# A decoder block on one core: the FFN's down projection as seven block products instead of eight, its left-hand sums made beside gate/up, and tiles aligned to 512 bytes

## The chip, the core and the metric

The kernel is one program for one core of a Trainium2 chip. The metric is device time of one execution in microseconds. All matrix products of the part that is changed are done in three passes: each f32 operand is split into a rounded part (`h`, type float32r) and the rest (`l`), and `h*h + h*l + l*h` is accumulated, so one 128x512 result of a contraction over 128 costs three matrix multiplications.

## The reference, cut to what matters

```
u = rms_norm(h, attn_norm_g);  h = h + hybrid_mixer(u, ...)      # two attention mixers, merged
u = rms_norm(h, ffn_norm_g)
h = h + (silu(u @ w_gate) * (u @ w_up)) @ w_down                 # 1024x1024 @ 1024x2816, then 1024x2816 @ 2816x1024
out = rms_norm(h, final_norm_g)
```

There are 1024 tokens, the model is 1024 wide and the FFN 2816 wide.

## The kernel before, in words

The kernel runs in stages: the attention mixers (until about 870 us), the branch projections and the output projection (until about 1047 us), the transposes that make the FFN's input (until about 1110 us), gate/up (until 1506 us), down (until 1748 us), and the last output tiles. A scheduler of the framework orders each engine's instructions by a simulated timeline; buffers in pools set how far a stage may run ahead. The order below the source is therefore not the order on the engines.

Gate/up (`Pair`, lines 1139 to 1221) is done already as 2x2x2 block products with seven multiplications: the tokens' halves and the model's halves of the input lie on chip as the eight tiles B11, B21, B22 and T1 to T4, and each `Pair` makes four results of 128 FFN columns x 512 tokens. `operand` (L1125) splits a block on ScalarE (L1128) and VectorE (L1129). What is gated, `sl` (L1183), goes to DRAM as `hhd`, 44 stores of 256 KB from GpSimd's queue (L1184). The two weights are loaded as `raw`, 128x8x256, rows of 1 KB (L1063).

Down (L1291 to L1329) is a plain product. Two halves of 512 tokens (`th`); in each, 22 steps over the FFN's 128-column slices. A step loads 128 rows of `w_down` (`wdr`, 512 KB) and the gated slice (`hr`, 256 KB), splits both (L1258 on ScalarE, L1259 on VectorE) and issues 24 matrix multiplications (L1308 to L1310) into all eight PSUM banks. Both halves load `w_down` anew. When a half is complete, the eight banks are added to the residual `hf` (L1318), the squares are summed (L1320), and the normalised tile is stored (L1327, L1329). `hf` has three buffers, so a fourth tile's load (L1314) waits until an earlier one's stores have landed.

The pools named `lined` pad each tile to a multiple of 128 bytes, and the pool `eps` at the right end of the memory holds 24 floats (96 bytes), which shifts all that lies left of it in right-hand pools. As allocated, the matrix multiplications of gate/up, down, branch and output projection have both operands at a remainder of 384 bytes to 512. Those of the merge gates and extra projections (`mg`, lines 314 to 338: 18 blocks x 2 halves x 24, 864 in all, 512 columns each) have the moving operand at remainder 384 and the stationary one at 0. The projections of 384 columns have 0 and 384.

## Time and profile before

| | us |
|---|---|
| median of 3 runs | 1773.97 (1773.64 to 9481.85) |
| profiled execution, device time | 1771.06 |
| its span | 1769.3 |
| granted TensorE clock, mean over the span | 0.982 |
| TensorE (PE) busy | 1681.4 (95%) |
| VectorE (DVE) busy | 1009.7 (57%) |
| ScalarE (ACT) busy | 753.5 (43%) |

The profile's page gives busy times over the whole span; a matrix multiplication is counted until its modelled end, so two that follow each other overlap in it, and the pace of a stage is read from the starts. Other views are the stretches (busy time and count of each engine between two times), the timeline of an engine, the groups of instructions, the chain of waits that ended last, and the DMA issues with the time until they landed. Times are from the span's start.

### The profile page before, as it was taken

Reading aid. Unit: us, or ns where it says so; the run is one execution under the profiler, and the core shown is the slowest. Engines: PE = TensorE matmul, PEld = TensorE weight load, DVE = VectorE, ACT = ScalarE, POOL = GpSimd, SP = SyncE. Lnnn points to the kernel's source line nnn. Section 1 sums busy time; section 2 is a strip of 40 time slices with the busy share of each in tenths; the row PEclk is TensorE's granted clock in tenths of the full one; section 3 lists DMA queues with packets and bytes.
Section 4 is the critical chain, followed back from the end, with each engine's and each line's share of the span. In section 5 each row is a group of like instructions: output and inputs, shape, how many; then the busy total and the mean of one; then the engine's idle time right before and its main releaser. Section 6 shows DMA issues by size and latency. Waiting matters only on the chain.

```text
span 1769.3 us, 24833 instructions
## 1 busy us (share of the span) xinstructions
PE 1681.4 (95%) x9157; PEld 1446.5 (82%) x9157; DVE 1009.7 (57%) x1974; ACT 753.5 (43%) x1574; POOL 436.5 (25%) x601
## 2 busy tenths in 40 slices
PE   5999999999999999999999988999999999998995
PEld 4888888887889989998888866888888888786884
DVE  8554645455358678888654177655555554335434
ACT  4334343344333268878643144433333332234323
POOL 4432323233122356657444020000000000001001
PEclk8999999999999999999999989999999999999998
DMA  6120211013223010100474320432222220545542
GB/s 204 45 78 24 78 44 58 30 47 106 73 74 87 14 31 26 39 16 21 145 246 150 107 95 30 137 107 84 78 95 72 78 96 36 196 143 178 174 144 82
DMA packets 120361, 157.90 MB, mean 89 GB/s; under 512 B 10208, under 2 KB 90112, under 8 KB 120240
## 3 DMA queue, kind: packets, MB, share of 16 engines
q1 hardware_dynamic: 111936, 132.50, 23.9%
q0 software_dynamic: 7120, 23.29, 3.4%
q8 instruction: 72, 1.18, 0.3%
q10 hardware_dynamic: 1184, 0.53, 0.1%
q14 instruction: 49, 0.40, 0.1%
HBM read 120.64 MB, written 35.65 MB: 88 GB/s over the span
## 4 chain that ended last, share of the span: by engine, by line
PE 84%; DVE 8%; ACT 4%; DMA 2%; issue 1%; POOL 1%; SPq 0%; ACTq 0%; DVEq 0%; POOLq 0%
PE mm L1135 8%; PE mm L1136 8%; PE mm L1137 8%; PE b L158 6%; PE b L159 6%; PE b L160 6%; PE s L874 3%; PE mm L1308 3%; PE mm L1309 3%; PE mm L1310 3%; PE b L927 3%; PE b L938 3%; PE s L158 2%; PE s L159 2%; PE s L160 2%; PE br L160 2%
## 5 line engine op out<-in xcount | busy, mean ns | idle before, releaser
L1184 POOL DMA_DIRECT2D hhd<-sl x44 | 23.9, 544 | 438.6 <-DVE sl L1183 438.6
L158 PE MATMUL b<-uh,mg_h 128*128 128x512 f32 x288 | 115.8, 402 | 0.7 <-ACT mg_st L337 0.7
L159 PE MATMUL b<-ul,mg_h 128*128 128x512 f32 x288 | 114.7, 398 | 0.0
L160 PE MATMUL b<-uh,mg_l 128*128 128x512 f32 x288 | 113.9, 395 | 0.0
L1128 ACT ACTIVATE oh<-S 128x512 fp32r<-128x512 f32 x88 | 55.6, 632 | 131.1 <-PE mm L1136 114.2
L874 PE MATMUL s<-kN,qN 128*128 128x320 f32 (+5 forms) x384 | 100.7, 365 | 3.6 <-ACT p L891 2.6
L1309 PE MATMUL mm<-wdl,hdh 128*128 128x512 f32 x264 | 102.7, 389 | 0.0
L1310 PE MATMUL mm<-wdh,hdl 128*128 128x512 f32 x264 | 102.5, 389 | 0.0
L1259 DVE TENSOR_TENSOR hdl<-hr,hdh 128x512 fp32r<-128x512 f32 x44 | 30.5, 692 | 120.1 <-ACT hdh L1258 117.3
L942 DVE TENSOR_TENSOR pl<-b,ph 128x512 fp32r<-128x512 f32 (+1 forms) x152 | 90.6, 613 | 12.8 <-ACT ph L941 11.8
L159 PE MATMUL b<-pw_l,uh 128*128 128x384 f32 x256 | 88.5, 346 | 6.6 <-DVE pw_l L269 6.6
L1258 ACT ACTIVATE hdh<-hr 128x512 fp32r<-128x512 f32 x44 | 27.8, 631 | 156.5 <-PE tp L1309 137.1
L941 ACT ACTIVATE ph<-b 128x512 fp32r<-128x512 f32 (+1 forms) x152 | 80.3, 545 | 31.7 <-PE b L938 30.4
L891 ACT ACTIVATE p<-s,mn 128x640 f32<-128x640 f32 (+7 forms) x128 | 89.3, 703 | 7.6 <-DVE sm L892 2.5
L158 PE MATMUL b<-pw_h,uh 128*128 128x384 f32 x256 | 89.7, 350 | 1.8 <-ACT uh L217 1.2
L898 POOL TENSOR_TENSOR p<-p,sm 128x640 f32<-128x640 f32 (+3 forms) x64 | 89.2, 1416 | 2.5
L160 PE MATMUL b<-pw_h,ul 128*128 128x384 f32 x256 | 88.4, 345 | 1.4 <-DVE ul L218 1.4
L1128 ACT ACTIVATE oh<-raw 128x512 fp32r<-128x512 f32 x66 | 41.6, 632 | 109.4 <-PE mm L1136 108.2
L1129 DVE TENSOR_TENSOR ol<-S,oh 128x512 fp32r<-128x512 f32 x88 | 60.4, 686 | 43.7 <-PE mm L1137 25.7
L938 PE MATMUL b<-ident,p 128*128 128x128 f32 x528 | 83.0, 275 | 1.4 <-POOL p L895 0.6
L465 DVE TENSOR_REDUCE mn<-s 128x1 f32<-128x128 f32 (+7 forms) x64 | 46.0, 753 | 55.4 <-PE s L464 55.3
L158 PE MATMUL s<-pw_h,uh 128*128 128x256 f32 (+1 forms) x256 | 74.9, 293 | 2.6 <-ACT xs L648 1.6
(387 smaller groups left out, 5187.8 us busy)
## 6 DMA issues: line engine op xcount, KB each, us to landing
wdr<-in_w_down_dram SPq DMA_DIRECT2D x44, 512.0 KB, 3.6
raw<-in_w_gate_dram SPq DMA_DIRECT2D x11, 1024.0 KB, 5.3
raw<-in_w_up_dram SPq DMA_DIRECT2D x11, 1024.0 KB, 5.3
hhd<-sl POOLq DMA_DIRECT2D x44, 256.0 KB, 2.3
hr<-hhd SPq DMA_DIRECT2D x44, 256.0 KB, 2.6
mg_raw<-in_w_in_dram SPq DMA_DIRECT2D x18, 512.0 KB, 4.6
mgd<-mg_st POOLq DMA_DIRECT2D x32, 256.0 KB, 3.7
sg<-mgd SPq DMA_DIRECT2D x16, 512.0 KB, 5.1
```

Source lines behind the costliest of these rows:

```text
L158: T.matmul(ps, ah, bh, start=(i == 0), stop=False)
L159: T.matmul(ps, ah, bl, start=False, stop=False)
L160: last = T.matmul(ps, al, bh, start=False, stop=(i == n - 1))
L874: T.matmul(s_[:, c], qN[:, 2 * hp + es[c * len(es) // 2], i * 128:(i + 1) * 128], kNs[br][:, v, g, c0:c0 + cw], start=(v == 0), stop=(v == 1))
L938: T.transpose(tp[:, 2 * (b - b0) + e], p[:, e, b * 128:(b + 1) * 128], ident)
L942: V.tensor_sub(pl[:, :nt], tp[:, :nt], ph[:, :nt])
L1128: A.activation(wh, src, AF.Copy)
L1135: T.matmul(ps, w[0][:, k], b[0][:, k], start=(first and k == 0), stop=False, **kw)
L1136: T.matmul(ps, w[0][:, k], b[1][:, k], start=False, stop=False, **kw)
L1137: T.matmul(ps, w[1][:, k], b[0][:, k], start=False, stop=(k == 3), **kw)
L1309: T.matmul(ps, hh[:, ts], dl[:, cs], start=False, stop=False)
L1310: T.matmul(ps, hl[:, ts], dh[:, cs], start=False, stop=(f == NF - 1))
```

## The change

Four things are done.

- **Down as seven block products.** The 1024x2816 gated matrix is cut into 2x2 blocks (token halves x FFN halves) and `w_down` into 2x2 blocks (FFN halves x column halves). Seven products of 11 steps each (`PRODUCTS`) are accumulated into two sets of four banks in turn, `bx` and `by`; a step splits one 128x512 piece of each side and issues 12 matrix multiplications. Partial results that two outputs share are copied out of PSUM by ScalarE (`kept`) and added later by VectorE (`settle`). The right-hand sums (`make`) are made on VectorE in place, in 33 of the 77 steps and for a later product.
- **The left-hand sums beside gate/up.** `gated_sums` makes S1 to S4 from the gated blocks, four VectorE operations for each of 11 pairs of `Pair`s, and stores seven blocks instead of four: 77 stores of 256 KB. For this a `Pair` takes FFN columns p and p+11, so `raw` is loaded in two DMAs with rows of 512 bytes.
- **`w_down` on chip.** Each of its four blocks is loaded once and stays: block 00 during gate/up, 01 and 11 into the place of B11 to B22, 10 into a pool of its own. The eight residual tiles `hf` are all on chip before the last products. The left-hand pieces `ar` come back from DRAM with two buffers.
- **Alignment.** `lined` pads to 512 bytes, `epst` holds 120 floats (480 bytes), small tiles of the first mixer go to a pool `das`. As allocated, both operands of the matrix multiplications named above are at remainder 0. The order of all engines up to the FFN's input stays the same.

The diff, cut to its core:

```diff
@@ -118,9 +118,9 @@
         def tile(self, shape, dtype, **kw):
             n = math.prod(shape[1:])
             size = 2 if dtype == BF else 4
-            if n * size % 128 == 0:
+            if n * size % 512 == 0:
                 return self.p.tile(shape, dtype, **kw)
-            t = self.p.tile([shape[0], -(-n * size // 128) * 128 // size], dtype, **kw)[:, :n]
+            t = self.p.tile([shape[0], -(-n * size // 512) * 512 // size], dtype, **kw)[:, :n]
...
-    epst = eps_pool.tile([128, 24], F32, name="epst")[:, 0:1]
+    epst = eps_pool.tile([128, 120], F32, name="epst")[:, 0:1]
...
             kT = st["kT", h]
-            mn = da.tile([128, 2], F32, name="mn")
-            sm = da.tile([128, 2], F32, name="sm")
-            rc = da.tile([128, 16], F32, name="rc")[:, 0:2]
+            mn = das.tile([128, 2], F32, name="mn")
+            sm = das.tile([128, 2], F32, name="sm")
...
 
-    hh_dram = [tc.dram_tile((128, S), F32, name="hhd%d" % i) for i in range(NF)]
+    HF = NF // 2
+    A_BLOCKS = ("A00", "A01", "A11", "S1", "S2", "S3", "S4")
...
         raws[n] = ffr.tile([128, KD, 256], F32, name="raw", bufs=2)
-        nc.sync.dma_start(raws[n], (w_gate, w_up)[b][:, p * 256:(p + 1) * 256].rearrange("(k p) n -> p k n", p=128))
+        for r in range(2):
+            c0 = (p + r * HF) * 128
+            nc.sync.dma_start(raws[n][:, :, r * 128:r * 128 + 128],
+                              (w_gate, w_up)[b][:, c0:c0 + 128].rearrange("(k p) n -> p k n", p=128))
...
     tres = fres.enter_context(ExitStack())
+    ff = ctx.enter_context(lined("ff", side="right"))
     tb_ = tres.enter_context(pool("tb", side="right"))
-    ff = tres.enter_context(lined("ff", side="right"))
     for nm in ("T1", "T2", "T3", "T4"):
         B[nm] = [tb_.tile([128, 4, 512], R, name="B%s%s" % (nm, v)) for v in "hl"]
 
     def operand(src):
-        wh = ff.tile([128, 4, 128], R, name="oh", bufs=4)
-        wl = ff.tile([128, 4, 128], R, name="ol", bufs=4)
+        wh = ff.tile([128, 4, 128], R, name="oh", bufs=6)
+        wl = ff.tile([128, 4, 128], R, name="ol", bufs=6)
         A.activation(wh, src, AF.Copy)
         V.tensor_sub(wl, src, wh)
...
             if not self.up:
-                sl = ff.tile([128, 512], F32, name="sl", bufs=5)
+                sl = gated_tile()
...
                 V.tensor_mul(sl, sl, ps if m is None else m)
-                nc.gpsimd.dma_start(hh_dram[2 * self.p + r][:, c * 512:(c + 1) * 512], sl)
+                self.gated_sums("A%d%d" % (c, r), sl)
+
+        def gated_sums(self, nm, t):
+
+            g = self.g
+            g[nm] = t
+
+            def store(k):
+                nc.gpsimd.dma_start(hh_dram[k][self.p], g[k])
+
+            if nm != "A10":
+                store(nm)
+            if nm == "A10":
+                g["S3"] = gated_tile()
+                V.tensor_sub(g["S3"], g["A00"], g["A10"])
+                store("S3")
+            elif nm == "A11":
+                g["S1"] = g["A10"]
+                V.tensor_add(g["S1"], g["A10"], g["A11"])
+                store("S1")
+                g["S2"] = gated_tile()
+                V.tensor_sub(g["S2"], g["S1"], g["A00"])
+                store("S2")
+            elif nm == "A01":
+                g["S4"] = gated_tile()
+                V.tensor_sub(g["S4"], g["A01"], g["S2"])
+                store("S4")
 
...
             self.done(1, 0, self.ps["X"], None)
+
+    late = []
+
+    def gated_tile():
+        if not late:
+            return ff.tile([128, 512], F32, name="sl0")
+        return late[0].tile([128, 512], F32, name="sl", bufs=7)
 
...
+    late.append(dn)
+    BW = {"00": [dn.tile([128, 512], F32, name="b00_%d" % p) for p in range(HF)]}
+
+    def load_block(nm, p):
+        r, c = int(nm[0]), int(nm[1])
+        nc.sync.dma_start(BW[nm][p], w_down[(p + r * HF) * 128:(p + r * HF + 1) * 128, c * 512:(c + 1) * 512])
...
             load_pair(n + 2)
+        if n >= NF - HF:
+            load_block("00", n - (NF - HF))
...
@@ -1288,45 +1318,131 @@
     tres.close()
 
 
...
+    dr = ctx.enter_context(pool("dr", side="right"))
+    quads = [ub.tile([128, 4, 512], F32, name="q" + nm, tag=nm)
+             for nm in ("B11h", "B11l", "B21h", "B21l", "B22h", "B22l")]
+    blocks = [t[:, i] for t in quads for i in range(4)]
+    BW["01"], BW["11"] = blocks[:HF], blocks[HF:2 * HF]
+    gO = flat(quads[5][:, 2:4])
+    BW["10"] = [dr.tile([128, 512], F32, name="b10_%d" % p) for p in range(HF)]
+    hf = [dr.tile([128, D], F32, name="hf%d" % t) for t in range(NT)]
+    ssq = dr.tile([128, NT, 2], F32, name="ssq")
+    bx = [fp.tile([128, 512], F32, name="tp", bufs=2) for _ in range(2)] + [mm_bank() for _ in range(2)]
+    by = [mm_bank() for _ in range(4)]
+
+    PRODUCTS = (("A00", "00", None, None, bx), ("S1", "00", ("01", "00"), "01", by),
+                ("S2", "00", ("11", "00"), "11", bx), ("S4", "11", None, None, by),
+                ("S3", "01", ("11", "01"), None, bx), ("A01", "10", None, "10", by),
+                ("A11", "00", ("10", "00"), None, bx))
+    GRP = 3
+    raw_a, ops = {}, {}
+    NS = len(PRODUCTS) * HF
+
+    def fetch(n):
+        i, p = divmod(n, HF)
+        if PRODUCTS[i][3]:
+            load_block(PRODUCTS[i][3], p)
+        raw_a[n] = dn.tile([128, 512], F32, name="ar", bufs=2)
+        nc.sync.dma_start(raw_a[n], hh_dram[PRODUCTS[i][0]][p])
+
+    def split(src):
+        h = ff.tile([128, 512], R, name="oh", bufs=6)
+        l = ff.tile([128, 512], R, name="ol", bufs=6)
+        A.activation(h, src, AF.Copy)
+        V.tensor_sub(l, src, h)
+        return h, l
+
+    def prepare(n):
+        i, p = divmod(n, HF)
+        _, nm, make, _, _ = PRODUCTS[i]
+        a = split(raw_a.pop(n))
+        w = BW[nm][p]
+        if make:
+            V.tensor_sub(w, BW[make[0]][p], BW[make[1]][p])
+        ops[n] = a + split(w)
+
+    def step(n, tbs):
+        i, p = divmod(n, HF)
+        ah, al, wh, wl = ops[n]
+        fresh = i in (0, 1, 5) and p == 0
+        kw = {} if i in (0, 1, 5) else dict(skip_group_check=True)
+        for tb in tbs:
+            ts = slice(tb * 128, (tb + 1) * 128)
+            ps = PRODUCTS[i][4][tb]
+            T.matmul(ps, ah[:, ts], wh, start=fresh, stop=False, **kw)
+            T.matmul(ps, ah[:, ts], wl, start=False, stop=False, **kw)
+            T.matmul(ps, al[:, ts], wh, start=False, stop=(p == HF - 1), **kw)
+
+    def kept(banks, places):
+        out_ = []
+        for tb in range(4):
+            pl, nm, bufs = places[tb]
+            out_.append(pl.tile([128, 512], F32, name=nm, bufs=bufs))
+            A.activation(out_[tb], banks[tb], AF.Copy)
+        return out_
+
+    def settle(t, c, bank_, part):
+
+        hc = hf[t][:, c * 512:c * 512 + 512]
+        if part is None:
+            V.tensor_add(hc, hc, bank_)
+        else:
+            V.tensor_add(part, bank_, part)
+            V.tensor_add(hc, hc, part)
+        sq = ff.tile([128, 512], F32, name="S", bufs=3)
+        A.activation(sq, hc, AF.Square, accum_out=ssq[:, t, c:c + 1])
+
+    def finish(t):
+        V.tensor_add(ssq[:, t, 0:1], ssq[:, t, 0:1], ssq[:, t, 1:2])
+        r = rsqrt(dr, [128, 1], ssq[:, t, 0:1], 1.0 / D, "fin")
+        rows = slice(t * 128, (t + 1) * 128)
+        h0, h1 = hf[t][:, 0:512], hf[t][:, 512:1024]
+        V.scalar_tensor_tensor(h0, h0, r, gO[:, 0:512], op0=OP.mult, op1=OP.mult)
+        nc.sync.dma_start(out[rows, 0:512], h0)
+        V.scalar_tensor_tensor(h1, h1, r, gO[:, 512:1024], op0=OP.mult, op1=OP.mult)
+        nc.sync.dma_start(out[rows, 512:1024], h1)
+
+    for n in range(2):
+        fetch(n)
+    prepare(0)
+    keep = {}
+    for n in range(NS):
+        i, p = divmod(n, HF)
+        if n + 2 < NS:
+            fetch(n + 2)
+        if n == HF:
+            nc.sync.dma_start(gO, bcast_rows(final_norm_g, D))
+        if i in (2, 4) and p < 4:
+            t = p + (0 if i == 2 else 4)
+            nc.sync.dma_start(hf[t], hx_dram[t])
+        if n + 1 < NS:
+            prepare(n + 1)
+        if n < NS - GRP:
+            step(n, range(4))
+        elif n == NS - 1:
             for tb in range(4):
...
+                for m in range(NS - GRP, NS):
+                    step(m, (tb,))
+                settle(tb + 4, 0, bx[tb], None)
+                finish(tb + 4)
+        if p < HF - 1:
+            continue
+        if i == 0:
+            keep["m1"] = kept(bx, [(dn, "sl", 7)] * 4)
+        elif i == 1:
+            keep["m5"] = kept(by, [(dn, "sl", 7)] * 3 + [(ff, "sl0", 1)])
+        elif i == 2:
+            keep["u2"] = kept(bx, [(dr, "u2d", 4)] * 4)
+        elif i == 3:
+            for tb in range(4):
+                settle(tb, 1, by[tb], keep["u2"][tb])
+        elif i == 4:
+            for tb in range(4):
+                settle(tb + 4, 1, bx[tb], keep["m5"][tb])
+        elif i == 5:
+            for tb in range(4):
+                settle(tb, 0, by[tb], keep["m1"][tb])
+                finish(tb)
```

Where the order of instructions moves, at three places that matter. First, SyncE's DMA queue as down begins. Before, after the last `raw` of gate/up (gO is the final gain, `hhd` the gated slices, `wdr` the rows of `w_down`):

```order
L1063 DMA raw<-in_w_up_dram 128x8x256
L1293 DMA gO<-in_final_norm_g_dram 128x1024
L1314 DMA hf<-hxd_11173 128x1024
L1314 DMA hf<-hxd_11174 128x1024
L1314 DMA hf<-hxd_11175 128x1024
L1253 DMA hr<-hhd_11156 128x512
L1251 DMA wdr<-in_w_down_dram 128x1024
L1253 DMA hr<-hhd_11157 128x512
```

Now, from the fifth step of the first product on (`ar<-A00d` are its left-hand pieces in order of steps, the first `qB22` rows load block 11, `b_0_15379` and those after it block 10; in the gap stand four more `hf` of the same size):

```order
L1346 DMA ar<-A00d_11159 128x512
L1414 DMA qB22l<-in_final_norm_g_dram 128x1024
L1289 DMA qB22h<-in_w_down_dram 128x512 x4
L1289 DMA qB22l<-in_w_down_dram 128x512 x2
L1346 DMA ar<-A00d_11160 128x512
L1346 DMA ar<-A00d_11161 128x512
L1417 DMA hf_15390<-hxd_11232 128x1024
...
L1346 DMA ar<-A00d_11162 128x512
...
L1417 DMA hf_15397<-hxd_11239 128x1024
L1289 DMA b_0_15379<-in_w_down_dram 128x512
L1346 DMA ar<-A00d_11163 128x512
```

Before, `hr` and `wdr` alternate behind three `hf`; now all eight `hf` and all of block 10 (ten more rows follow, four before the next `ar` and six before the one after it) stand ahead of the pieces for the last three steps of the first product, two products before they are used.

Second, VectorE where a set of banks is complete. Before, at the end of the first half of the tokens:

```order
L1259 TENSOR_TENSOR wdl<-wdr,wdh 128x1024
L1318 TENSOR_TENSOR hf<-hf,mm 128x512 x6
L1323 TENSOR_TENSOR ss<-ss 128x1
L1259 TENSOR_TENSOR hdl<-hr,hdh 128x512
```

Now, at the end of the fourth product (`u2d` is what was kept of the third; `qB11h` is the right-hand side of the fifth):

```order
L1352 TENSOR_TENSOR ol<-qB11h,oh 128x512
L1390 TENSOR_TENSOR u2d<-mm,u2d 128x512 x3
L1391 TENSOR_TENSOR hf_15390<-hf_15390,u2d 128x512
L1390 TENSOR_TENSOR u2d<-mm,u2d 128x512
L1391 TENSOR_TENSOR hf_15391<-hf_15391,u2d 128x512
L1352 TENSOR_TENSOR ol<-ar,oh 128x512
L1352 TENSOR_TENSOR ol<-qB11h,oh 128x512
```

Two steps of the next product are split ahead of the additions, and six additions stand ahead of the third step's split.

Third, VectorE at the very end. Before, from the last split on:

```order
L1259 TENSOR_TENSOR wdl<-wdr,wdh 128x1024
L1318 TENSOR_TENSOR hf<-hf,mm 128x512 x5
L1323 TENSOR_TENSOR ss<-ss 128x1
L1318 TENSOR_TENSOR hf<-hf,mm 128x512
...
L1328 SCALAR_TENSOR_TENSOR hf<-hf,fin_r,gO 128x512
L1318 TENSOR_TENSOR hf<-hf,tp 128x512 x2
L1323 TENSOR_TENSOR ss<-ss 128x1
```

Now:

```order
L1352 TENSOR_TENSOR ol<-b_10_12219,oh 128x512
L1388 TENSOR_TENSOR hf_15394<-hf_15394,tp 128x512
...
L1388 TENSOR_TENSOR hf_15397<-hf_15397,mm 128x512
L1396 TENSOR_TENSOR ssq<-ssq 128x1 x2
...
L1400 SCALAR_TENSOR_TENSOR hf_15394<-hf_15394,fin_r,qB22l 128x512
L1402 SCALAR_TENSOR_TENSOR hf_15394<-hf_15394,fin_r,qB22l 128x512
...
L1402 SCALAR_TENSOR_TENSOR hf_15397<-hf_15397,fin_r,qB22l 128x512
```

Eight additions, the last two of them behind a load, have become four, one for each bank; the scaling of both halves of a row, four tiles, is VectorE's, eight operations where it had four.

## Rows read from the trace of the kernel before

**Rows 1.** The page: busy time of the engines, and the chain that ended last, by engine.
```profile
PE 1681.4 (95%) x9157; PEld 1446.5 (82%) x9157; DVE 1009.7 (57%) x1974; ACT 753.5 (43%) x1574; POOL 436.5 (25%) x601
PE 84%; DVE 8%; ACT 4%; DMA 2%; issue 1%; POOL 1%; SPq 0%; ACTq 0%; DVEq 0%; POOLq 0%
```
**Rows 2.** Stretches: from:to, length, busy us (count) by engine, granted clock, DMA share, GB/s.
```profile
200.00:400.00 200.00, 198.31 (x1107) 175.18 (x1106) 104.03 (x254) 77.77 (x203) 59.50 (x99) 1.00 0.18 54
963.00:980.00 17.00, 17.00 (x77) 14.08 (x76) 3.06 (x5) 2.90 (x8) 0.00 (x0) 1.00 0.92 339
1100.00:1500.00 400.00, 398.62 (x1770) 329.84 (x1768) 215.86 (x334) 150.74 (x256) 22.23 (x41) 1.00 0.26 85
1506.20:1747.70 241.50, 232.84 (x1016) 191.20 (x1014) 96.38 (x126) 79.13 (x115) 7.02 (x6) 0.99 0.48 157
```
**Rows 3.** Line L1308, one of down's three: instructions, ns min/median/max, first and last start.
```profile
L1308 PE MATMUL mm<-wdh,hdh x264: 389/389/501, 1491.4 to 1743.4; 128*128 128x512 f32 x132
L1308 PE MATMUL tp<-wdh,hdh x88: 389/389/795, 1126.9 to 1743.8; 128*128 128x512 f32 x88
```
**Rows 4.** Timeline of PE: start us, duration us; gate/up, then turns in down.
```profile
1299.67 0.39 PE L1135 MATMUL mm<-BT2h,oh 128*128 128x512 f32 x1
...
1301.48 0.39 PE L1137 MATMUL mm<-B11h,ol 128*128 128x512 f32 x1
...
1506.16 0.39 PE L1137 MATMUL mm<-BT4h,ol 128*128 128x512 f32 x1
1507.33 0.50 PE L1308 MATMUL mm<-wdh,hdh 128*128 128x512 f32 x1 [0.78 <-DVE sl L1183]
...
1626.58 0.39 PE L1310 MATMUL mm<-wdh,hdl 128*128 128x512 f32 x1
1633.37 0.80 PE L1308 MATMUL tp<-wdh,hdh 128*128 128x512 f32 x1 [6.41 <-DVE hf L1318]
...
1636.93 0.40 PE L1310 MATMUL tp<-wdh,hdl 128*128 128x512 f32 x1
...
1747.47 0.39 PE L1310 MATMUL tp<-wdh,hdl 128*128 128x512 f32 x1
```
**Rows 5.** The chain that ended last, its end: start us, us, what.
```profile
1754.35 4.03 DMA hf<-hxd
...
1758.45 0.70 DVE hf L1318
...
1762.55 0.72 ACT hf L1325
```
**Rows 6.** Groups of 1500 to 1769 us by form: count, busy us, mean ns, idle before.
```profile
L1259 DVE TENSOR_TENSOR wdl<-wdr,wdh 128x1024 fp32r<-128x1024 f32 x42 | 51.4, 1225 | 13.0 <-ACT wdh L1258 13.0
L1259 DVE TENSOR_TENSOR hdl<-hr,hdh 128x512 fp32r<-128x512 f32 x42 | 29.1, 693 | 119.8 <-ACT hdh L1258 117.0 <-PE mm L1309 1.5 <-PE tp L1309 1.3
L1258 ACT ACTIVATE hdh<-hr 128x512 fp32r<-128x512 f32 x42 | 26.5, 631 | 156.5 <-PE tp L1309 137.1 <-PE mm L1309 15.9 <-issue 3.6
L1318 DVE TENSOR_TENSOR hf<-hf,mm 128x512 f32<-128x512 f32 x12 | 7.4, 682 | 5.1 <-PE mm L1310 5.1
L1328 DVE SCALAR_TENSOR_TENSOR hf<-hf,fin_r,gO 128x512 f32<-128x512 f32 x8 | 6.0, 749 | 0.2
```
**Rows 7.** DMA issues over the span: count, KB each, median us from issue to landing.
```profile
raw<-in_w_up_dram SPq DMA_DIRECT2D x11, 1024.0 KB, 5.3
hr<-hhd SPq DMA_DIRECT2D x44, 256.0 KB, 2.6
mg_raw<-in_w_in_dram SPq DMA_DIRECT2D x18, 512.0 KB, 4.6
```
**Rows 8.** Tile `hr`, its loads: shortest, median and longest time to landing.
```profile
DMA to landing us min/median/max: 2.5/2.6/8.2
```
**Rows 9.** Timeline of PE in a merge-gate unit: start us, duration us.
```profile
390.09 0.39 PE L159 MATMUL b<-ul,mg_h 128*128 128x512 f32 x1
...
395.20 0.40 PE L160 MATMUL b<-uh,mg_l 128*128 128x512 f32 x1
```

More of the change, by code (lines that the diff above doesn't have):

```diff
@@ L146, in hybrid_block @@
     G.tensor_copy(identb, ident)
+    nlam = const.tile([128, 32], F32, name="nlam")[:, 0:1]
     with pool("masks") as mkp:
@@ L230, in hybrid_block @@
     gsub = ac.tile([128, 128], F32, name="gsub")
-    nlam = ac.tile([128, 32], F32, name="nlam")[:, 0:1]
     work = early.enter_context(pool("work", bufs=2))
@@ L403, in hybrid_block @@
                 mg_done[0] = 1
-    with pool("da", bufs=2) as da:
+    with pool("da", bufs=2) as da, pool("das", bufs=2) as das:
         def d_project(n):
@@ L524, in lam_scalar @@
             lp = da.tile([128, 2, HD], F32, name="lp", bufs=1)
-            ls = da.tile([128, 32], F32, name="ls", bufs=1)[:, 0:2]
+            ls = das.tile([128, 2], F32, name="ls", bufs=1)
             V.tensor_mul(lp, lam[:, 0:4:2, :], lam[:, 1:4:2, :])
@@ L1048, in blocks_pool @@
         return ctx.enter_context(pool(name, **kw))
-    hh_dram = [tc.dram_tile((128, S), F32, name="hhd%d" % i) for i in range(NF)]
+    HF = NF // 2
+    A_BLOCKS = ("A00", "A01", "A11", "S1", "S2", "S3", "S4")
+    hh_dram = {nm: [tc.dram_tile((128, 512), F32, name="%sd%d" % (nm, i)) for i in range(HF)] for nm in A_BLOCKS}
     hx_dram = [tc.dram_tile((128, D), F32, name="hxd%d" % i) for i in range(NT)]
@@ L1245, in hybrid_block @@
     dn = ctx.enter_context(pool("dn"))
-    steps = {}
-    def load_down(n):
-        th, f = divmod(n, NF)
-        wr = dn.tile([128, D], F32, name="wdr", bufs=2)
-        nc.sync.dma_start(wr, w_down[f * 128:(f + 1) * 128, :])
-        hr = dn.tile([128, 512], F32, name="hr", bufs=3)
-        nc.sync.dma_start(hr, hh_dram[f][:, th * 512:(th + 1) * 512])
-        out_ = []
-        for nm, raw, w in (("wd", wr, D), ("hd", hr, 512)):
-            h = dn.tile([128, w], R, name=nm + "h", bufs=2)
-            l = dn.tile([128, w], R, name=nm + "l", bufs=2)
-            A.activation(h, raw, AF.Copy)
-            V.tensor_sub(l, raw, h)
-            out_ += [h, l]
-        steps[n] = out_
+    late.append(dn)
[3 more added lines that the diff above has]
+        nc.sync.dma_start(BW[nm][p], w_down[(p + r * HF) * 128:(p + r * HF + 1) * 128, c * 512:(c + 1) * 512])
     load_pair(2)
```

47 lines of the change are left out of this document (5 added, 42 removed).

## The prediction

> **What bounds the kernel now.** I read the chain of waits first, then the stretches, then single turns on the timeline. TensorE is 84% of the chain that ended last and busy 95% of the span [rows 1]; in the stretch of the first mixer it is busy 198 of 200 us, in gate/up 398.6 of 400 [rows 2]. So a matrix multiplication that disappears, or comes sooner after the last one, is time saved almost one for one, and work on other engines costs only where it makes TensorE wait. The pace is read from starts: in gate/up eight intervals of 512 columns take 1301.48 - 1299.67 = 1.81 us, 0.2265 us each [rows 4]. Down is different only in that it has visible holes: the starts jump from 1626.58 to 1633.37 where the second half of the tokens needs banks that VectorE must first empty, and after the last start at 1747.47 there follow 21.8 us without any [rows 4].
>
> **Down's multiplications.** Before, each of three lines issues 264 + 88 = 352 [rows 3], 1056 in all. After, 7 products x 11 steps x 12 = 924. 132 fewer x 0.2265 = **-29.9 us**, all on the path.
>
> **The holes in down.** Between 1506.20 and 1747.70 lie 241.5 us with 1016 starts, the last of gate/up's drain included, so 1014 of down [rows 2]; 1014 x 0.2265 = 229.7, which leaves 11.8 us of holes. The largest is named above, 6.79 - 0.23 = 6.6 us; the eight intervals after it take 1636.93 - 1633.37 = 3.56 us instead of 1.81, 1.7 us more, slow until the pace returns; entering down costs 1.17 - 0.23 = 0.9 us [rows 4]. The change removes their causes: one set of four banks fills while the other is emptied, and the first product's steps are placed among gate/up's last ones. **-11.8 us**. What is late next at such a turn is VectorE, which has two steps split (5.4 us for TensorE) and six additions of 0.68 us ahead of the third step's two splits of 0.69 us: 4.1 + 1.4 = 5.5 us [rows 6]. It starts early, since the first bank is complete before its step ends, so I charge **+1 us** for all turns together, between 0 and 8 (5.5 us behind nothing, at one and a half turns).
>
> **VectorE and ScalarE in a step.** Before, a step of 24 multiplications (5.44 us) cost VectorE 1.225 + 0.693 us. Now one of 12 (2.72 us) costs 2 x 0.693 for the splits, and in 33 of 77 a right-hand sum, which I take at 0.69 like the splits: at most 2.1 of 2.72 us; ScalarE 2 x 0.631 [rows 6]. Both fit, VectorE at three quarters instead of about a third. In the last product the first four tiles' scaling (eight of 0.749), the settling of the fifth (eight of 0.682), 22 splits and some small operations come to about 30 us against 132 x 0.2265 = 29.9: cover just gone, counted in the +1.
>
> **Gate/up.** Four sums per 168 multiplications (38 us) add 4 x 0.69 = 2.8 us to a VectorE that is busy 216 of 400 us [rows 2]; hidden. 33 more stores only need GpSimd's queue, which does nothing else there. `raw` now comes as two transfers of 512 KB with 512-byte rows: the load of exactly this form, `mg_raw`, lands in 4.6 us against 5.3 for the 1 MB form [rows 7]; two in a row, some 9 us, against about 17 us in which the other buffer is used. Hidden; 0. Loads of pieces that the scheduler has put ahead of `raw` on SyncE's queue wait for stores made a pair earlier; 0.
>
> **Loads at the start of down.** This is the cost that I do put in. Behind the last use of B22 SyncE's queue issues the gain (0.5 MB), six pieces of block 11 (1.6), eight `hf` (4.2) and block 10 (2.9), and the pieces of the first product's steps 5 to 10 stand among them (1.6): 10.8 MB. The fastest long stretch moved 339 GB/s at 92% of the DMA engines [rows 2]: 31.9 us. TensorE needs the last of these pieces when step 10 begins, 132 multiplications after B22's end = 29.9 us, less 1.3 us for the two splits [rows 6] and the hand-offs: 28.4 us. And the queue is not always full, since a piece's load waits until its buffer of two is split. So the last pieces are late by 31.9 - 28.4 = 3.5 us and a little: **+5 us**. Ends: 0, where the loads spread better; 11, where two pieces in turn land as late as the latest `hr` did, 8.2 instead of 2.6 us [rows 8]. The Trainium skill ("DMA: Bandwidth & Descriptors", queues, rings and completion order) says that each DMA engine consumes a ring's descriptors in order, which speaks against the change: a small urgent load cannot pass a bulk one. Its limit per core of 358 GB/s would make it 10.8 / 0.358 = 30.2 us, 2 us late, and the sum 3 us lower; the row's 339 decides.
>
> **The tail.** Before, 1769.3 - 1747.47 = 21.8 us: eight banks, and the fourth tile waits 4.03 us for its load after a store [rows 4, 5]. After, the last bank is added (0.68 us) 0.3 us after the last start; squares, sums and the root's chain about 3 us more; then four scalings (3.0), the second pair's small operations (about 1.4) and four more scalings (3.0) [rows 6]: 11.4 us to the last result. Before, the last result came at 1762.55 + 0.72 = 1763.27, 6.0 us before the span's end [rows 5]; with one store fewer to issue after it, 5.5. Together 16.9: **-4.9 us**; between -2 and -8.
>
> **Alignment.** In a merge-gate unit 22 intervals take 395.20 - 390.09 = 5.11 us, 0.2323 each [rows 9], 5.8 ns more than gate/up's 0.2265 [rows 4] for the same 512 columns. The two differ in where the operands lie: remainders 384 and 0 to 512 in the first, 384 and 384 in the second. The change gives both remainder 0 everywhere. If equal remainders are what counts, 864 x 5.8 ns = **-5.0 us**; gate/up and down stay. Ends: 0, and -7, with 768 projections of 384 columns gaining 2 ns each as well. The Trainium skill ("SBUF — State Buffer", its section on two separate sides) holds that TensorE has read ports of its own and never waits for anyone there, and calls the start rule one of legality, not of speed. By it this term is 0; the trace shows the two paces, though not yet their cause.
>
> **Sum**, against the profiled execution's 1771.06: -29.9 - 11.8 + 1 + 5 - 4.9 - 5.0 = -45.6, **1725.5 us**. The median of the runs, 1773.97, is 2.9 us higher, and a kernel after would stand to its own median likewise; I say 1727.
>
> **Rivals.**
> - *The alignment does nothing.* For it: the merge gates run beside other work than gate/up does, and a pace may have other causes. Against: branch and gate/up stages have different neighbours too and one pace. 1727 + 5 = 1732. Chance 0.18. This is the outcome by the page on SBUF of the Trainium skill, named above.
> - *Down is paced by its supply for longer than the start.* The bulk loads cost the full 11 and the turns 8: 1727 + 6 + 7 = 1740, and up to 1755 if a gap is followed by slow multiplications as the one before 1633 is [rows 4]. For it: VectorE's share doubles and it is a queue in order. Against: two steps of reserve. 0.18.
> - *The two buffers of `ar` set the pace throughout, and it gets slower than before.* A buffer's cycle is landing, ScalarE's split, VectorE's, and hand-offs: 2.6 + 0.63 + 0.69 + 0.3 (my estimate) = 4.2 us for two steps, under the 5.44 that TensorE needs [rows 6, 7]. It decides from a landing of 3.8 us on. At the 5.3 us of `raw` [rows 7] it is 6.9 us for two steps, 3.46 x 77 = 266 instead of 209 us: +57, **1784**. Against: after the start only 0.26 MB per step are moved, 96 GB/s. 0.05.
> - *Remainder 0 is as bad as unequal ones.* Then 3540 multiplications of 512 columns (gate/up 1848, down 924, branch and output 768) gain 5.8 ns instead: 1727 + 5 + 20 = 1752. 0.04.
> - *More is won:* no late loads, and the smaller multiplications of the mixers run closer too: 1727 - 5 - 1 - 9 = 1712 or less. 0.08.
>
> My forecast's own case (1717 to 1738) has the rest, 0.47. Two per cent, about what a measurement of this kernel can tell from no change, is 35.5 us: under 1738.5 is faster. That takes the forecast, the first rival, nearly all of the last and a little of the second: 0.47 + 0.17 + 0.08 + 0.02 = 0.74, which I lower to 0.71 for what I have not seen; slower, above 1809, 0.02; the rest 0.27. The range leaves out the third rival, the fourth, part of the second and the lower part of the last: 1710 to 1748.
>
> **What would show it.** 924 starts in down at 0.2265 us; no jump of several us at the turns from one product to the next; short waits of TensorE for `ol` or `oh` in the last three steps of the first product, ended by a DMA into `ar`; about 17 us from the last start to the end; merge-gate units at 0.2265 us an interval. I am wrong if TensorE waits for `ar` in the later products (third rival), if gate/up's 0.2265 changes (fourth), or if gate/up has holes, in which case the sums or the 512-byte rows were not hidden.

## The result, and the profile after

The changed kernel takes **1728.6 us** (median of 4 executions, 1727.7 to 1730.0) against 1773.8 (now a median of four); the ratio is 0.9751, 95% interval 0.9738 to 0.9763. The forecast was 1727. The profiled execution took 1729.99 us, its span is 1728.3, so the span is 41.0 us shorter.

Page of the changed kernel: busy times, and the chain that ended last, by engine.

```profile
PE 1648.4 (95%) x9025; PEld 1422.4 (82%) x9025; DVE 1088.0 (63%) x2148; ACT 769.7 (45%) x1644; POOL 441.9 (26%) x626
PE 80%; DVE 8%; issue 5%; ACT 3%; DMA 3%; POOL 2%; SPq 0%; DVEq 0%; ACTq 0%; POOLq 0%
```

132 matrix multiplications fewer, as written; VectorE has 78 us more work and is still not the bound. Down, as stretches of the changed kernel (from:to, length, then busy us and count of TensorE's multiplications (PE), its weight loads (PEld), VectorE (DVE), ScalarE (ACT) and GpSimd (POOL), granted clock, DMA share, GB/s):

```profile
1505.90:1715.60 209.70, 204.76 (x890) 168.80 (x889) 139.84 (x240) 98.91 (x185) 1.08 (x2) 0.98 0.42 138
1506.00:1536.00 30.00, 25.06 (x98) 20.14 (x97) 18.90 (x31) 8.53 (x16) 1.08 (x2) 0.89 0.88 335
1656.00:1686.00 30.00, 30.00 (x134) 24.88 (x133) 18.94 (x32) 15.51 (x31) 0.00 (x0) 1.00 0.32 98
```

Two of the 890 are gate/up's last. From its last start at 1505.95 to down's last at 1715.36 are 888 intervals and 209.4 us; at 0.2267 us these are 201.3, so 8.1 us are holes, where before there were 11.5 to 11.8 [rows 2, 4]. All of them lie in the first 30 us: TensorE starts 98 multiplications there instead of 134, at a mean granted clock of 0.89 and with the DMA engines at 0.88. Every later stretch looks like the third one, product turns included. The one place, on TensorE's timeline:

```profile
1505.95 0.39 PE L1142 MATMUL mm<-BT4h,ol 128*128 128x512 f32 x1
...
1519.55 0.39 PE L1374 MATMUL mm<-oh,ol 128*128 128x512 f32 x1
1524.88 1.22 PE L1372 MATMUL tp<-oh 128*128 128x512 f32 x2 [4.94 <-ACT oh L1351]
1525.89 1.05 PE L1372 MATMUL mm<-oh 128*128 128x512 f32 x2
```

The chain of waits says what `oh` waited for (start us, us, what):

```profile
1500.67 4.28 DMA ar<-A00d
...
1506.44 7.84 DMA ar<-A00d
...
1514.36 9.21 DMA ar<-A00d
...
1524.21 0.62 ACT oh L1351
```

and SyncE's queue shows what stood ahead of those pieces (start us, time of all in the row):

```profile
1503.68 1.85 SPq L1417 DMA_DIRECT2D hf<-hxd  x2
1506.44 0.32 SPq L1346 DMA_DIRECT2D ar<-A00d  x1
1506.86 3.96 SPq L1417 DMA_DIRECT2D hf<-hxd  x6
1513.05 0.33 SPq L1289 DMA_DIRECT2D b<-in_w_down_dram  x1
1514.36 0.32 SPq L1346 DMA_DIRECT2D ar<-A00d  x1
```

A piece issued at 1514.36, behind six `hf` and a piece of block 10, landed 9.21 us later. The DMA issues over the whole span show that this is the first product alone (count, KB each, median us to landing):

```profile
raw<-in_w_up_dram SPq DMA_DIRECT2D x22, 512.0 KB, 4.6
...
hf<-hxd SPq DMA_DIRECT2D x8, 512.0 KB, 9.9
...
ar<-A00d SPq DMA_DIRECT2D x11, 256.0 KB, 5.1
...
ar<-S1d SPq DMA_DIRECT2D x11, 256.0 KB, 2.6
```

A merge-gate unit of the changed kernel: 22 intervals take 391.58 - 386.57 = 5.01 us, 0.2277 each instead of 0.2323 [rows 9].

```profile
386.57 0.39 PE L160 MATMUL b<-ul,mg_h 128*128 128x512 f32 x1
...
391.58 0.39 PE L161 MATMUL b<-uh,mg_l 128*128 128x512 f32 x1
```

The tail: TensorE's last start, then VectorE's first additions and its last scaling.

```profile
1715.36 0.39 PE L1374 MATMUL mm<-oh,ol 128*128 128x512 f32 x1
```
```profile
1714.43 1.29 DVE L1388 TENSOR_TENSOR hf<-hf,tp 128x512 f32<-128x512 f32 x2 [4.77 <-PE tp L1374]
...
1724.39 0.75 DVE L1402 SCALAR_TENSOR_TENSOR hf<-hf,fin_r,qB22l 128x512 f32<-128x512 f32 x1
```

From the last start to the end of the span are 12.9 us where there were 21.8 [rows 4, 5].

### The profile page after: what moved, and what is told of

Its sections match the earlier page's. It is cut to its first block, busy times and chain, and to the rows that moved or that the text cites. A ratio compares the mean times of both kernels' runs of the same rounds, so it can differ in the third digit from the quotient of the medians.

```text
span 1728.3 us, 25058 instructions
## 1 busy us (share of the span) xinstructions
PE 1648.4 (95%) x9025; PEld 1422.4 (82%) x9025; DVE 1088.0 (63%) x2148; ACT 769.7 (45%) x1644; POOL 441.9 (26%) x626
## 4 chain that ended last, share of the span: by engine, by line
PE 80%; DVE 8%; issue 5%; ACT 3%; DMA 3%; POOL 2%; SPq 0%; DVEq 0%; ACTq 0%; POOLq 0%
PE mm L1140 8%; PE mm L1141 8%; PE mm L1142 8%; PE b L159 5%; PE b L160 5%; PE b L161 5%; PE b L927 3%; PE s L874 3%; PE mm L1372 3%; PE mm L1373 3%; PE mm L1374 3%; PE b L938 3%; PE s L159 2%; PE s L160 2%; PE s L161 2%
## 5 line engine op out<-in xcount | busy, mean ns | idle before, releaser
L942 DVE TENSOR_TENSOR pl<-b,ph 128x512 fp32r<-128x512 f32 (+1 forms) x152 | 90.6, 613 | 12.3 <-ACT ph L941 11.2
L1351 ACT ACTIVATE oh<-ar 128x512 fp32r<-128x512 f32 x77 | 48.6, 632 | 106.5 <-PE mm L1373 72.8
L1352 DVE TENSOR_TENSOR ol<-ar,oh 128x512 fp32r<-128x512 f32 x77 | 53.3, 692 | 66.2 <-ACT oh L1351 62.6
L941 ACT ACTIVATE ph<-b 128x512 fp32r<-128x512 f32 (+1 forms) x152 | 80.2, 544 | 31.3 <-PE b L938 29.9
L1373 PE MATMUL mm<-ol,oh 128*128 128x512 f32 x220 | 86.2, 392 | 0.0
L1374 PE MATMUL mm<-oh,ol 128*128 128x512 f32 x220 | 86.1, 391 | 0.0
L1134 DVE TENSOR_TENSOR ol<-S,oh 128x512 fp32r<-128x512 f32 x88 | 59.6, 687 | 29.9 <-ACT oh L1133 25.6
L927 PE MATMUL b<-ph,vN 128*128 128x256 f32 x264 | 75.1, 302 | 0.0
```

Source lines behind the costliest of these rows:

```text
L927: T.matmul(o, lhsT, rhs, start=(done == 0), stop=(done == total - 1))
L1373: T.matmul(ps, ah[:, ts], wl, start=False, stop=False, **kw)
L1374: T.matmul(ps, al[:, ts], wh, start=False, stop=(p == HF - 1), **kw)
```

## Experiments

Each was timed beside the kernel before on the same chip, and the chips differ by 0.2% (its median was 1772.1, 1775.5 and 1772.1 us in the three groups of runs), so ratios are to be compared, not times. The changed kernel's is 0.9751.

### 1. The bulk loads later

```diff
-        nc.sync.dma_start(raw_a[n], hh_dram[PRODUCTS[i][0]][p])
+        keep["ar"] = nc.sync.dma_start(raw_a[n], hh_dram[PRODUCTS[i][0]][p])
+        if i == 4:
+            with tc.issue_after(keep["ar"].ins):
+                load_block("10", p)
...
-            nc.sync.dma_start(hf[t], hx_dram[t])
+            with tc.issue_after(keep["ar"].ins):
+                nc.sync.dma_start(hf[t], hx_dram[t])
```

> The changed kernel with the eight hf tiles and the eleven pieces of block 10 moved back on SyncE's queue, each behind a piece ar of the product before the one that uses it (hf in the third and fifth product, block 10 in the fifth). Theory: the one stall of down, 5.33 us at the ninth step of the first product, and the 13 multiplications of 0.426 us behind it (13 x 0.2 = 2.6 us) come from ar pieces that stand behind 7 MB of bulk loads in the queue; without them 1728.6 - 5.1 - 2.6 = about 1721 us, and TensorE busy 30.0 of 30 us in the stretch 1506 to 1536. Rival (two buffers of ar are too few whenever anything else is on the queue): the stall comes back at the third and fifth product, where hf and block 10 are now loaded between pieces, and the time stays at 1726 to 1732 us. Second rival (the stall is VectorE's, which makes sums for other products in the first one): nothing changes, 1728 to 1729 us.

**1720.6 us, ratio 0.9710 (0.9697 to 0.9722)**: 0.41% of before's time, 7.3 us, under the changed kernel, where 7.7 were expected. In the trace no interval of down is above 0.6 us and none is slow:

```profile
1506.00:1536.00 30.00, 30.00 (x134) 24.86 (x133) 26.54 (x42) 14.20 (x26) 1.08 (x2) 1.00 0.39 128
1626.00:1656.00 30.00, 30.00 (x134) 24.73 (x133) 23.27 (x38) 15.38 (x30) 0.00 (x0) 1.00 0.55 170
```

The same megabytes now go in two other products (DMA share 0.55) without any wait; VectorE is busier in the first stretch than it was beside the stall (26.5 against 18.9 us), so it was not the cause. Both rivals fall. This version beats both kernels.

### 2. The same bunch elsewhere

On the version of 1, all `hf` and block 10 behind the fifth piece of the third product:

```diff
+        if n == 3 * HF - 7:
+            with tc.issue_after(keep["ar"].ins):
+                for t in range(NT):
+                    nc.sync.dma_start(hf[t], hx_dram[t])
+                for q in range(HF):
+                    load_block("10", q)
```

> The kernel with the late bulk loads, but all eight hf and the eleven pieces of block 10, 7.1 MB, in one bunch in the queue behind the fifth piece of the third product, where the next piece must follow them. Theory (a piece waits for what stands ahead of it in its queue, wherever that is, and two pieces of reserve cover about 9 us): 7.1 MB at the 339 GB/s seen are 20.9 us, so one stall of about 12 us (10 to 14) in the third product, 13 slow multiplications behind it (2.6 us), and no stall in the first: 1720.6 + 14.6 = 1735 us (1732 to 1738). Rival (the stall belongs to the start of down, where gate/up's last stores, loads and splits coincide): no stall in the third product, 1721 us.

One execution: **1732.8 us**, 12.2 above experiment 1 at the same median of before. Waits of TensorE in down, and SyncE's queue:

```profile
PE tp L1378 <- ACT oh L1357: 11.0, 1, 11.0
```
```profile
1556.79 4.48 SPq L1350 DMA_DIRECT2D hf<-hxd  x8
1561.31 11.47 SPq L1289 DMA_DIRECT2D b<-in_w_down_dram  x11
1573.10 6.90 SPq L1346 DMA_DIRECT2D ar<-S2d  x3
```

The stall moved with the bunch: 11.2 us (12 expected), 12 slow multiplications behind it, none in the first product. From 1556.79 until the piece behind the bunch could be split (TensorE goes on at 1579.50, 1.3 us after it) are 21.4 us; 7.1 MB at 339 GB/s gave 20.9. SyncE needs 11.5 us to issue the eleven loads, where a single one took 0.33 us in the changed kernel, and issues the next piece only behind them, at 1573.10. That something ahead of SyncE was full is my reading and not shown. The rule of the Trainium skill ("DMA: Bandwidth & Descriptors", queues, rings and completion order) that a ring is consumed in order fits a piece that cannot pass the loads ahead of it; this trace, in which most of the delay falls before the piece is issued, does not test it.

### 3. The pieces on another queue

```diff
-        nc.sync.dma_start(raw_a[n], hh_dram[PRODUCTS[i][0]][p])
+        nc.gpsimd.dma_start(raw_a[n], hh_dram[PRODUCTS[i][0]][p])
```

> The changed kernel with the pieces ar loaded from GpSimd's queue; the bulk loads (gain, blocks, hf) stay on SyncE's queue and now wait for no piece at all. Theory (order within one queue: a piece cannot pass the bulk loads issued ahead of it): the pieces land in about 3 to 5 us, the stall at the ninth step is gone, 1728.6 - 7.7 = 1721 us. Rival (the DMA engines are simply full while 9 MB are loaded, whichever queue asks): the pieces land in 8 us or more as before, and the stall of 5 us stays or grows, 1728 us or more, since the bulk loads now start sooner. Second rival (the pieces now stand behind the last stores of gated blocks on GpSimd's queue): a wait at the first step of down instead, of a few us.

1725.1 us, **ratio 0.9724 (0.9704 to 0.9745)**: between the two, though its interval overlaps both of theirs a little. The trace separates them. Stretch and waits:

```profile
1506.00:1536.00 30.00, 28.24 (x119) 21.73 (x119) 22.38 (x36) 12.04 (x22) 5.48 (x11) 1.00 0.91 353
```
```profile
PE tp L1372 <- ACT oh L1351: 1.4, 3, 0.9
```

The long stall is gone, but 15 multiplications of 134 are still missing from the 30 us (3.4 us; 36, or 8.2 us, in the changed kernel), and the pieces of the first product land in a median of 5.4 us, not less than the 5.1 there. No wait stands at the first step of down, so the second rival falls. Neither of the other two holds alone: order in the queue makes the one long wait, and busy DMA engines (0.91, 353 GB/s) keep the pieces slow whichever queue asks. Moving the bulk in time cures both, moving the pieces to another queue one.

### 4. One buffer for the pieces

```diff
-        raw_a[n] = dn.tile([128, 512], F32, name="ar", bufs=2)
+        raw_a[n] = dn.tile([128, 512], F32, name="ar", bufs=1)
```

and each piece fetched one step ahead, on the version of 1.

> The kernel with the late bulk loads and one buffer for ar instead of two, each piece fetched one step ahead. It measures the cycle of a buffer on which the third rival of the forecast rested: landing 2.6 + split on ScalarE 0.63 + on VectorE 0.69 + hand-offs 0.3 = 4.2 us. If that is right every step of down takes 4.2 instead of 2.72 us, 77 x 1.5 = +114 us, about 1835 us, and TensorE waits 1.5 us for oh or ol in each step. If the cycle is really 5.4 us or more (the third rival's condition, two buffers without reserve): 1720.6 + 77 x 2.7 = 1930 us or more. If TensorE runs slow after each short wait, more again.

One execution: **1826.9 us**, +106 where +114 was expected. The pieces' issues in the second product:

```profile
L1346 SPq DMA_DIRECT2D ar<-S1d x11: 319/320/320, 1532.3 to 1573.1; - x11
```

From the first of eleven issues to the last are 40.8 us, 4.08 us a cycle (4.35 in the sixth product); the estimate was 4.2. Two buffers therefore last for two steps, 5.44 us, with 1.2 us to spare while pieces land in 2.6 us. That is why the third rival did not come, and also why a landing of 8 us broke it at once. From 1506 to 1706 a wait of about 1.4 us in each step, 2.3 at most, did not make TensorE slow: the granted clock stays at 1.00. Behind two later waits it does not (a stretch, columns as above):

```profile
1706.00:1806.00 100.00, 75.94 (x280) 53.16 (x279) 49.57 (x99) 34.68 (x69) 0.00 (x0) 0.95 0.28 87
```

After a wait of 2.5 us at 1735.10 six multiplications take 0.427 us each, after one of 1.7 us at 1767.15 thirteen. So short waits are not always free, and the length of a wait alone does not tell what follows it.

### 5. Alignment alone, products alone

The first keeps before's down; the second is the changed kernel with the lines that pad to 512 bytes, `epst`, `nlam` and `das` put back.

```diff
-            if n * size % 128 == 0:
+            if n * size % 512 == 0:
...
-    epst = eps_pool.tile([128, 24], F32, name="epst")[:, 0:1]
+    epst = eps_pool.tile([128, 120], F32, name="epst")[:, 0:1]
```

> The kernel before with the alignment alone (rows padded to 512 bytes, epst 480 bytes, nlam in the constants, small tiles of the first mixer in a pool of their own); down stays a plain product. Theory: unequal remainders of the two operands cost 5.8 ns a multiplication of 512 columns in the merge gates, so 864 x 5.8 ns = 5.0 us go there and part of it is lost again in the branch stage: 1769 to 1772 us against 1773.8, the merge gates' intervals at 0.227 us. Rival (alignment does nothing, the pace of the changed kernel comes with something else in it): 1773.8 us, intervals at 0.232. Rival (alignment changes only which buffers are free when): a change of either sign with the intervals at 0.232.

> The changed kernel without the alignment (rows padded to 128 bytes, epst 96 bytes, the small tiles where they were before). Theory: the block products alone give 1728.6 + 1 to 4 = 1730 to 1733 us, the merge gates back at 0.232 us an interval, the last merge-gate multiplication about 4.7 us later than in the changed kernel. Rival (the alignment carries more than that, also in down or gate/up): 1738 us or more, and gate/up's intervals above 0.2265.

Alignment alone: 1769.0 us, **ratio 0.9983 (0.9974 to 0.9991)**, 3.1 us. Products alone: 1732.9 us, **0.9781 (0.9768 to 0.9793)**, 0.30% or 5.3 us above the changed kernel. The mean interval of a merge-gate multiplication, over 821 of them that follow each other within 0.3 us, is 232.8 ns before, 232.9 with products alone, 228.7 with alignment alone and 228.7 in the changed kernel; in gate/up and down it is 226.8 in all four. So the alignment acts on the merge gates, where the forecast put it, but takes 4.1 of the forecast's 5.8 ns off; the projections of 384 columns gain 1.6 ns (178.5 before, 176.9 in the changed kernel), gate/up and down nothing. The traces agree from run to run: from the 201st merge-gate multiplication to the last, the two kernels without alignment take 323.0 us and all eleven with it 319.1 to 319.6. Products alone lies 5.3 us above the changed kernel where 1 to 4 were expected, alignment alone 3.1 us under the kernel before.

### 6. Operands at unequal remainders in gate/up

```diff
-    epst = eps_pool.tile([128, 120], F32, name="epst")[:, 0:1]
+    epst = eps_pool.tile([128, 24], F32, name="epst")[:, 0:1]
```

> The changed kernel with epst at 24 floats again and all else as in it: tiles in right-hand pools start at remainder 384 to 512, those in left-hand pools at 0. The 792 multiplications of gate/up that read B11, B21 or B22 then have the moving operand at 0 and the stationary one at 384; the 1056 that read T1 to T4, all of down (but not the branch projections, 0 and 0) have 384 and 384. Theory (unequal remainders are what counts, whichever operand is off): those 792 take 0.232 us instead of 0.2265, +4.6 us, 1733 us, and within gate/up the two kinds differ. Rival (only a moving operand off 0 beside a stationary one at 0 is slow, as in the merge gates before): 1728.6 us, both kinds 0.2265. Rival (any remainder other than 0 is slow): gate/up and down slow throughout, 3540 x 5.8 ns = +20 us at most.

1735.3 us, **ratio 0.9792 (0.9779 to 0.9805)**, 0.41% slower than the changed kernel. One passage of its gate/up shows both kinds:

```profile
1297.69 0.39 PE L1140 MATMUL mm<-BT4h,oh 128*128 128x512 f32 x1
...
1303.13 0.40 PE L1140 MATMUL mm<-B22h,oh 128*128 128x512 f32 x1
...
1305.69 0.39 PE L1142 MATMUL mm<-B22h,ol 128*128 128x512 f32 x1
```

24 intervals with 384 and 384 take 5.44 us, 0.2267 each; the 11 that follow with 0 and 384 take 2.56, 0.2327. Over all of gate/up the means of those under 0.3 us are 227.4 and 232.6 ns, where the changed kernel has 226.8 and 227.0. A remainder of 384 is as good as 0 if both operands have it, and it does not matter which of them is off. From gate/up's first start to its last this kernel takes 5.7 us longer than the changed one; 792 x 5.7 ns are 4.5 of it, the rest I have not followed.

The same with 56 floats, so that the right-hand tiles lie at 256:

> The changed kernel with epst at 56 floats: tiles in right-hand pools at remainder 256 to 512, left-hand ones at 0. Read within gate/up alone: multiplications that read B11, B21, B22 have operands at 0 and 256, those that read T1 to T4 have 256 and 256. If equality counts modulo 512: 0.232 us for the first kind, 0.227 for the second, and a time near 1735 us as with 384. If it counts modulo 256 or less: 0.227 us for both, 1728 to 1729 us.

One execution, 1731.8 us beside a median of before of 1775.5; that is 0.9754 beside the changed kernel's 0.9751. The same passage:

```profile
1297.06 0.39 PE L1140 MATMUL mm<-BT4h,oh 128*128 128x512 f32 x1
...
1302.49 0.39 PE L1140 MATMUL mm<-B22h,oh 128*128 128x512 f32 x1
...
1305.21 0.39 PE L1140 MATMUL mm<-B11h,oh 128*128 128x512 f32 x1
```

5.43 us for 24 and 2.72 for 12: 0.226 and 0.227; over all of gate/up the two kinds have 226.8 and 226.9 ns. Operands at 0 and 256 run as fast as equal ones. What has to be equal is the remainder to 256 bytes, as far as 0, 256 and 384 tell it; by that, padding to 256 would have done, which no run tried.

### 7. The tail

Three versions of experiment 1's kernel. In the first, GpSimd multiplies the last four tiles' second halves by the gain at the end of the fifth product, and ScalarE scales them at the end:

```diff
+        if c == 1 and t >= 4:
+            G.tensor_mul(hc, hc, gO[:, 512:1024])
...
+        if t >= 4:
+            A.activation(h1, h1, AF.Copy, scale=r)
+        else:
```

> The kernel with the late bulk loads (1720.6 us), and the last four tiles' second halves multiplied by the gain on GpSimd as soon as they are complete, at the end of the fifth product, and scaled by the root on ScalarE; VectorE scales four first halves at the end instead of eight halves. Theory (VectorE's scalings, 0.66 us each, are what the tail consists of after the roots): four fewer, 1720.6 - 2.65 = 1718.0 us. Rival (the tail is set by the chain of roots and ScalarE's squares): 1720 us. Second rival (GpSimd's work at the end of the fifth product takes VectorE's port or delays settling, and TensorE waits there): slower than 1720.6 us.

**0.9707 (0.9691 to 0.9723)**, no difference from experiment 1. The last result is ready 7.4 us after the last start instead of 9.8, nearly the 2.65 us expected, but the end comes only 1.0 us sooner, 11.9 instead of 12.9: the last store is issued 8.0 us after the last start, not 7.4, since eight stores now leave within about 4 us, and from its issue to the end it is 3.9 us instead of 3.1. And what the second rival names happened, though it did not make the kernel slower than experiment 1. GpSimd and VectorE at the end of the fifth product:

```profile
1649.89 1.52 POOL L1398 TENSOR_TENSOR hf<-hf,qB22l 128x512 f32<-128x512 f32 x1 [140.13 <-ACT S L1396]
```
```profile
1650.17 1.79 DVE L1355 TENSOR_TENSOR ol<-ar,oh 128x512 fp32r<-128x512 f32 x1
...
1654.78 0.68 DVE L1355 TENSOR_TENSOR ol<-ar,oh 128x512 fp32r<-128x512 f32 x1
```

A split beside GpSimd's multiplication takes 1.79 us, without it 0.68, and TensorE waits 0.7 us for `ol`. The Trainium skill ("SBUF — State Buffer", who interferes with whom) has this as an exclusive lock on a port pair that the two share; the trace agrees, with 1.79 us against 0.68.

In the second, GpSimd multiplies the first halves after their last addition, as the kernel before does:

> The kernel with the late bulk loads (1720.6 us), and the last four tiles' first halves multiplied by the gain on GpSimd right after their last addition and scaled by the root on ScalarE, as the kernel before did it. VectorE again has four scalings at the end, so the last result comes 2 to 2.6 us sooner. Theory (the program's end waits for a drain of GpSimd, which in the kernel before ended at 1768.56, 7.3 us after GpSimd's last operation; in the changed kernel GpSimd works on nothing at the end): the drain ends 7 us after the fourth product on GpSimd, that is about 3.5 us (its start after the first addition) + 4 x 1.3 us + 7.3 us after the last matmul's start at the latest, so the end does not come sooner in spite of the sooner result: 1720 to 1723 us, 2 us or more above the variant with GpSimd's work done early. Rival (the drain is short when GpSimd is done, and the 2.1 us of the program's end came from something else): as the early variant, 1718 us.

0.9704 (0.9687 to 0.9720), by its time no different from experiment 1. My theory fell: in the trace the tail is 14.3 us instead of 12.9, not because of a drain, which ended 1.1 us after GpSimd's last operation, but because VectorE's small operations were held up by GpSimd's four products:

```profile
1708.08 4.93 POOL L1400 TENSOR_TENSOR hf<-hf,qB22l 128x512 f32<-128x512 f32 x4 [197.94 <-ACT S L1396]
```
```profile
1710.77 2.26 DVE L176 SCALAR_TENSOR_TENSOR fin_t<-fin_r,fin_a 128x1 f32<-128x1 f32 x2
```

The third puts the multiplications on VectorE, one in each of four steps of the sixth product:

```diff
+        if i == 5 and 4 <= p < 8:
+            with tc.issue_after(keep["ol"].ins):
+                V.tensor_mul(hf[p][:, 512:1024], hf[p][:, 512:1024], gO[:, 512:1024])
```

> The kernel with the late bulk loads (0.971 of before), and the last four tiles' second halves multiplied by the gain on VectorE, one in each of four steps of the sixth product, and scaled by the root on ScalarE at the end; GpSimd does nothing there. Theory (in the variant with GpSimd the tail was 1.0 us shorter, 11.9 instead of 12.9 us after the last start, and what ate it were waits of TensorE for VectorE's splits while GpSimd worked): the tail is 11.9 us again and TensorE does not wait, 1.0 us below the late bulk loads alone, about 0.9704 of before. Rival (the last stores bound the tail): no change of the tail, 0.971. Second rival (four more operations make VectorE late in the sixth product): waits of TensorE for ol there.

1720.4 us, **0.9708 (0.9695 to 0.9721)**. In the trace it is as expected, 11.8 us of tail and one wait for `ol`:

```profile
PE tp L1376 <- DVE ol L1355: 0.2, 1, 0.2
```

The 1 us is too small for the timing to confirm. The eight stores are issued back to back here, over 4.1 us, so the tail is by then bound by the stores as the trace reads; no run tests it.

## Why the prediction was right, point by point

| step of the forecast | forecast | measured |
|---|---|---|
| 132 multiplications fewer | -29.9 | -29.9 (924 starts, pace 226.8 ns) |
| holes of down gone | -11.8 | -11.5, all of the old ones |
| gate/up's sums and 512-byte rows | 0 | 0: no interval above 0.6 us from 1112 to 1505 |
| turns between products | +1 | 0: no wait at any of them |
| late pieces at the start of down | +5 | +8.1: a stall of 5.1 us, one interval of 0.59 us, and 13 multiplications of 0.426 us behind it, +2.6 |
| the tail | -4.9 | -9.0 |
| alignment | -5.0 | -4.7 at the last merge gate: 3.5 from the merge gates, 1.2 from 384 columns |
| branch and FFN-input stages | not in the sum | +1.3 (0 to +1.6 in the other aligned runs) and +3.5 |

- **The mechanisms were right**; the sizes of the late pieces and of the tail were not, alignment came to its size out of two parts, and one stage was left out. That the time was met closer than the terms is luck: their errors have both signs. The last step has no working either: 1725.5 and the 2.9 us named beside it are 1728.4, not 1727. And it took for granted that the two profiled executions stand alike to their medians: before's lay 2.8 us under it, after's 1.4 over. Between profiled executions the gain is 41.1, between medians 45.2, against a sum of 45.6.
- **Late pieces.** Place, cause and wait itself were as written (5.1 against 5). The step that was mis-sized is that it priced the wait alone, though the slow multiplications after a hole stood in the rows [rows 4] and in the second rival. The stretch's granted clock of 0.89 shows them, behind a wait of 5.1 us. 0.426 us an interval is the lower of its two levels, 1.2 GHz (512 / 1.2 = 427 ns).
- **The tail.** 1.6 of the missing 4.1 us are VectorE's: its scalings follow each other every 0.66 us where I put 0.75 [rows 6], and the small operations of two tiles overlap. 2.4 are the program's end: in the trace of before the last store is done at 1766.2, but GpSimd's drain, issued behind its last product, ends only at 1768.6, and the end waits for it. After, GpSimd has long been idle, and its part of the end follows SyncE's at once. Why that drain took 7.3 us there and 1.1 us in experiment 7 stays open.
- **Alignment.** First rival (it does nothing) and fourth (0 as bad as unequal) are out, by experiments 5 and 6. But the step that took all 5.8 ns for the alignment's was too large: 864 x 4.1 ns are 3.5 us, and merge-gate units at 0.2265 us, one of the signs, did not come (0.2277 in the unit shown). More than a quarter of the aligned merge gates' intervals still take 230 to 237 ns; why stays open. The other 1.2 us are the 768 projections of 384 columns, 1.6 ns each, which stood only in the range. The last merge gate itself starts between 495.7 and 500.2 us in the eleven aligned runs, so the -4.7 of one pair of executions is a weak measure. The rule of the Trainium skill that I weighed against it ("SBUF — State Buffer", who interferes with whom: TensorE never waits on anyone) says nothing of where an operand starts, and what the page has under operand start alignment is about legality and comes from runs that timed nothing; so neither makes this term 0, and the measured interval decides.
- **What was not in the sum.** Adding up the intervals of TensorE above 0.6 us, less 0.23 each, the FFN-input stage (1045 to 1112 us) has 12.3 us of holes before and 12.4 with alignment alone, but 15.7 with products alone and 15.8 in the changed kernel. So it belongs to the products. VectorE's order around the transposes is another there; which of its steps costs the time I have not separated. I costed gate/up and not the stage that leads into it. Waits of the changed kernel in that stage; before, the first was 3.5 us and the second absent:

```profile
PE tp L1081 <- DVE hx L1112: 4.7, 1, 4.7
...
PE tp L1081 <- DVE BT3l L1083: 1.7, 1, 1.7
```

- **The third rival** (two buffers set the pace) had the right cycle, 4.1 to 4.4 us measured for its 4.2, and the right reason against it. **The second** came true in its smaller half. VectorE's share of down rose to 67% (139.8 of 209.7 us) and never set the pace.

## What to carry to other kernels

When a change brings everything on chip early, look at where in the same queue the small urgent loads stand: a 7 MB bunch cost stalls of 5 and 11 us at the two places where it was put, and none when one bulk load went behind each piece. Price a stall of TensorE with the slow multiplications that follow it. Where long float32r multiplications run at two paces in one kernel, compare the start addresses of their two operands; here that was 4 of the 6 ns between the two paces.

## What the runs showed of the hardware that I had not expected

- The pace of a 512-column float32r multiplication depended on whether both operands started at the same remainder to 256 bytes: in gate/up 0.227 us for 0 and 0, 384 and 384, 256 and 256, 0 and 256, and 0.233 us for 0 and 384; in the merge gates 0.233 us for 384 and 0 and 0.229 for 0 and 0.
- Waits of about 1.4 us in every step left the granted clock at 1.00 for 200 us; waits of 5.1 and 11.2 us were followed by 13 and 12 multiplications at half the pace, but one of 6.6 us in the kernel before by seven, and one of 1.7 us in experiment 4 by thirteen.
- A VectorE split of 0.68 us took 1.77 to 1.79 us beside a GpSimd multiplication of the same size, and two operations on one column 2.26 us.
- The loads at the start of down moved 335 GB/s as a mean of 30 us, and 353 when the pieces came from another queue; a 256 KB load in the midst of it landed in 5 to 9 us instead of 2.6.
